# A hybrid decoder layer on one core: gate and up with another order of the seven products, longer lead of the adding transfers and one weight sum on VectorE

## Chip, cores and metric

One core of a Trainium2 chip. The metric is the device time of one execution of the whole kernel, in microseconds (us).

## The reference

One decoder layer over 512 tokens of width 2048, in float32. RMSNorm, an input projection, four token mixers side by side (two kinds of attention, a gated unit, RWKV-7), an output projection and a residual; then the part that the change is about, RMSNorm and a SwiGLU feed-forward of width 5632, and a final RMSNorm:

```python
def swiglu(h, w_gate, w_up, w_down):
    return (jax.nn.silu(h @ w_gate) * (h @ w_up)) @ w_down
...
        x = x + ycat.reshape(B, S, D_MIX) @ w_out[l]
        h = rmsnorm(x, norm_ffn_g[l])
        x = x + swiglu(h, w_gate[l], w_up[l], w_down[l])
    return rmsnorm(x, norm_final_g)
```

## The kernel before

Every product of float32 matrices is made of three matmuls on float32r parts: high times high, high times low, low times high. The high part is a rounded copy that ScalarE writes, the low part is what VectorE gets when it subtracts the high part from the value. `split2` (L1047, L1048) does both.

**Gate and up** are one product of 2 x 2 blocks in Strassen's manner (Winograd's form): the two halves of the tokens by the two halves of the model width, times the two halves of the width by gate and up. Seven products P1 to P7 stand for eight. Their activation operands (`cmb`) are sums of the four blocks of the normalised residual, made once while the output projection ends: `make_x2` adds the residual, `first_sums` and `last_sums` make sums and split them, `square_x2` and `add_squares` collect the squares for the norm, and what is not done by then comes from the generators `late_sums` and `ffn_norm`. The width of 5632 is worked in 11 groups (`gi`) of 512 columns of gate and of up. A group has 28 steps: seven products in the order of `ORDER` by four pieces `jj` of the inner dimension. A step is 2 inner tiles by 2 token tiles by 3 matmuls.

The weights' side is made as the products go. The queue of SP loads 512 KB pieces into X[jj] (tile T, four buffers, `w_dma`) for P1 and 256 KB pieces (tile wq) for P3 and P2. The sums of weight blocks that P5, P6, P4 and P7 need are made by transfers that add (`accum_op`), issued on POOL's queue by `w_add`: into X[jj] for P5, P6 and P4, into the raw tiles of P3 for P7. Each can start when the product before it on that tile has been split. `w_split` cuts a step's weight into high and low, `w_next` issues transfers and a split in order, `w_ahead` keeps the splits two steps ahead of the matmuls and the loads some steps more.

Products gather in PSUM. P6, P7 and P4 add onto the bank of P1, P3 adds onto that of P5, P2 has its own (`strassen`, dictionary `bank`). After the last matmul of a product `got_product` copies or adds the bank into tiles c11, c12, c21, c22. When gate and up of a token half are there it hands them to `turn_h`, a generator that gates (Silu by ScalarE, a product by VectorE), turns the result by transposes on TensorE, forms the operands of the down projection and stores them to DRAM from ScalarE's queue (`put`). Generators in `side` go one step on at each half-step of the matmuls (`run`, `step_side`), so where a `yield` stands decides beside which matmuls a piece of gating is issued. All engines work through their instructions in the order of issue.

The order before is P1 P5 P6 P3 P7 P4 P2. **The down projection** follows; two of its products are issued ahead of what is left of the gating, and its tiles take over the memory of the stage before.

## Time and profile before

| | us |
|---|---|
| median of 3 runs | 2351.08 |
| lowest and highest run | 2344.31, 2355.11 |
| the profiled execution | 2343.19 |
| span of the profiled execution, first to last instruction | 2341.5 |
| mean granted clock of TensorE over the span | 0.987 |

The times of single instructions below come from the profiled execution. A matmul's duration overlaps with those of its neighbours; its pace is the distance from start to start. The time that an engine sat idle before an instruction, and what ended it, stand behind the instruction.

### The profile page before, as it was taken

What the parts mean: (1) busy time and instruction counts of PE and PEld (TensorE: products, weight loads), DVE (VectorE), ACT (ScalarE), POOL (GpSimd) and SP (SyncE); (2) the same over time, 40 slices, a digit from 0 to 9 for tenths busy, and PEclk for the clock granted to TensorE, in tenths of its full rate; (3) what the DMA queues carried; (4) which work ended last, traced back from release to release, by engine and by line L of the source; (5) the groups of instructions that cost most, each with busy time, mean ns of one, the idle gap of its engine ahead of it and who ended that gap; (6) DMA issues with size and microseconds to landing.
All of it is one profiled execution on the core that took longest, in us unless ns stands there. A gap on an engine that the chain in (4) does not pass through costs nothing.

```text
span 2341.5 us, 29080 instructions
## 1 busy us (share of the span) xinstructions
PE 2240.9 (96%) x11064; PEld 1788.6 (76%) x11064; DVE 1357.1 (58%) x1950; ACT 1010.6 (43%) x1508; POOL 194.3 (8%) x236
## 2 busy tenths in 40 slices
PE   8999999999999997999999999999999889999996
PEld 6788878877777775777777777777777668888884
DVE  6555456654444456755555455555555577777775
ACT  5522222244444444544454454444445344443333
POOL 0000000000000000212211221221221100000000
PEclk9999999999999999999999999999999989999998
DMA  5232323122233334877977987797797587547884
GB/s 185 83 98 73 102 68 100 61 91 84 69 106 106 95 113 140 183 189 181 259 196 177 235 209 185 200 246 185 188 257 195 137 304 239 173 124 259 286 308 153
DMA packets 164541, 388.92 MB, mean 166 GB/s; under 512 B 29296, under 2 KB 34928, under 8 KB 164400
## 3 DMA queue, kind: packets, MB, share of 16 engines
q1 hardware_dynamic: 103728, 245.15, 31.8%
q0 software_dynamic: 31680, 92.29, 21.2%
q10 hardware_dynamic: 28992, 49.61, 6.1%
q8 instruction: 87, 1.43, 0.2%
q14 instruction: 54, 0.44, 0.1%
HBM read 348.93 MB, written 38.05 MB: 165 GB/s over the span
## 4 chain that ended last, share of the span: by engine, by line
PE 56%; issue 17%; DMA 12%; DVE 7%; ACT 4%; POOL 3%; ACTq 0%; SPq 0%; POOLq 0%; DVEq 0%
DMA T<-in_wgu_dram 8%; PE acc L145 7%; PE acc L147 7%; PE acc L146 7%; PE bk L1379 5%; PE bk L1380 5%; PE bk L1378 5%; PE acc L166 3%; PE acc L168 2%; PE acc L167 2%; DMA wq<-in_wgu_dram 2%; POOL wq L1141 2%; PE prod L1294 2%; PE prod L1295 2%; PE prod L1296 2%
## 5 line engine op out<-in xcount | busy, mean ns | idle before, releaser
L1048 DVE TENSOR_TENSOR wl<-T,wh 128x1024 fp32r<-128x1024 f32 x176 | 214.8, 1224 | 267.8 <-ACT wh L1047 265.5
L1295 PE MATMUL prod<-wl,h 128*128 128x512 f32 x704 | 278.3, 395 | 15.2 <-DVE wl L1048 14.6
L1047 ACT ACTIVATE wh<-T 128x1024 fp32r<-128x1024 f32 x176 | 185.9, 1059 | 236.4 <-DMA T<-in_wgu_dram 117.9
L1294 PE MATMUL prod<-wh,h 128*128 128x512 f32 x704 | 276.0, 392 | 1.6 <-ACT wh L1047 1.6
L1296 PE MATMUL prod<-wh,l 128*128 128x512 f32 x704 | 274.7, 390 | 0.0
L1378 PE MATMUL bk<-dh,ah 128*128 128x512 f32 x608 | 239.4, 394 | 25.0 <-ACT dh L1047 25.0
L1048 DVE TENSOR_TENSOR wl<-wq,wh 128x512 fp32r<-128x512 f32 x264 | 173.1, 689 | 135.4 <-ACT wh L1047 134.5
L1379 PE MATMUL bk<-dl,ah 128*128 128x512 f32 x608 | 239.5, 394 | 3.3 <-DVE dl L1048 3.3
L107 DVE TENSOR_TENSOR wlo<-wraw,whi 128x1024 fp32r<-128x1024 f32 x127 | 155.3, 1222 | 148.2 <-ACT whi L106 147.9
L1380 PE MATMUL bk<-dh,al 128*128 128x512 f32 x608 | 238.2, 392 | 0.0
L106 ACT ACTIVATE whi<-wraw 128x1024 fp32r<-128x1024 f32 x127 | 133.9, 1054 | 196.5 <-PE acc L146 94.1
L145 PE MATMUL acc<-xhi,whi 128*128 128x512 f32 x512 | 209.6, 409 | 5.4 <-ACT whi L121 5.1
L1047 ACT ACTIVATE wh<-wq 128x512 fp32r<-128x512 f32 x264 | 155.2, 625 | 134.7 <-PE prod L1296 75.2
L1143 POOL DMA_DIRECT2D T<-in_wgu_dram x132 | 118.1, 917 | 1140.9 <-DVE x L1036 588.5
L147 PE MATMUL acc<-xhi,wlo 128*128 128x512 f32 x512 | 201.1, 393 | 1.2 <-DVE wlo L107 1.2
L146 PE MATMUL acc<-xlo,whi 128*128 128x512 f32 x512 | 200.8, 392 | 0.3 <-DVE xlo L239 0.3
L1295 PEld LDWEIGHTS prod<-wl,h 128*128 128x128 f32 x704 | 132.1, 188 | 55.7 <-DVE wl L1048 29.0
L1294 PE MATMUL prod<-wh,hb 128*128 128x512 f32 x352 | 142.1, 404 | 18.7 <-DVE c L1265 18.7
L1294 PEld LDWEIGHTS prod<-wh,h 128*128 128x128 f32 x704 | 132.2, 188 | 31.5 <-ACT wh L1047 4.1
L1378 PEld LDWEIGHTS bk<-dh,ah 128*128 128x128 f32 x608 | 115.3, 190 | 50.5 <-ACT dh L1047 26.7
L1296 PEld LDWEIGHTS prod<-wh,l 128*128 128x128 f32 x704 | 132.2, 188 | 26.6
L1047 ACT ACTIVATE dh<-T 128x1024 fp32r<-128x1024 f32 x66 | 70.0, 1060 | 172.5 <-DVE T L1457 56.3
(315 smaller groups left out, 4128.6 us busy)
## 6 DMA issues: line engine op xcount, KB each, us to landing
rw<-in_wdn_dram SPq DMA_DIRECT2D x134, 512.0 KB, 4.9
T<-in_wgu_dram POOLq DMA_DIRECT2D x132, 512.0 KB, 9.6
wq<-in_wgu_dram SPq DMA_DIRECT2D x176, 256.0 KB, 5.7
wraw<-in_wi_dram SPq DMA_DIRECT2D x63, 512.0 KB, 3.6
T<-in_wgu_dram SPq DMA_DIRECT2D x44, 512.0 KB, 5.1
wq<-in_wgu_dram POOLq DMA_DIRECT2D x88, 256.0 KB, 9.1
wraw<-in_wt_dram SPq DMA_DIRECT2D x32, 512.0 KB, 3.6
wraw<-in_wo_dram SPq DMA_DIRECT2D x32, 512.0 KB, 3.6
```

The lines of the kernel that those rows point to most:

```text
L107: dv.tensor_sub(lo, r, hi.bitcast(F32))
L145: pe.matmul(acc[b], wh, xh, start=(c == 0 and k == 0), stop=False)
L146: pe.matmul(acc[b], wh, xl, start=False, stop=False)
L147: pe.matmul(acc[b], wl, xh, start=False, stop=(c == nchunk - 1 and k == 3))
L1047: ac.activation(hi, src, AF.Copy)
L1048: dv.tensor_sub(lo, src, hi.bitcast(F32))
L1294: pe.matmul(acc[t], ah[:, tt], hi[:, u], start=first, stop=False, skip_group_check=more)
L1295: pe.matmul(acc[t], ah[:, tt], lo[:, u], start=False, stop=False, skip_group_check=more)
L1296: pe.matmul(acc[t], al[:, tt], hi[:, u], start=False, stop=(j == 7), skip_group_check=more)
L1378: pe.matmul(o, ah[:, a], hi[:, cc], start=fresh, stop=False, skip_group_check=True)
L1379: pe.matmul(o, ah[:, a], lo[:, cc], start=False, stop=False, skip_group_check=True)
L1380: pe.matmul(o, al[:, a], hi[:, cc], start=False, stop=last, skip_group_check=True)
```

## The change

The products of gate and up run in the order P1 P2 P5 P3 P6 P7 P4. P6's weight sum is no longer a transfer: after P3's split VectorE adds P3's raw tiles to X. The transfers that add are issued 8 steps ahead of the split instead of 4, the loads 7 steps ahead of the matmuls instead of 8. P2 and P5 have banks of the pool `px`, P1 one of `pm`. c11 is complete after P2, c12 after P6, c22 after P7, c21 with P4, so that the first token half is gated beside P7 and the second beside P1 and P2 of the next group; `turn_h` makes and stores the operands of the down projection in another order and keeps the first half's blocks until the second half is there. On the activations' side the sums are split in interleaved pieces (`first_high`, `a11_high` and so on), the lower blocks (`lower_half`) come before the `last_sums`, and `ffn_norm` begins ten half-steps later.

```diff
-    def split_a11(j):
-        a11 = t2("a11", dt=F32R)
-        split2(a11[:, lo_t], xg[j][:, lo_t], a11[:, hi_t])
+    def a11_high(j):
+        a11 = cmb["P1", j] = t2("a11", dt=F32R)
+        ac.activation(a11[:, lo_t], xg[j][:, lo_t], AF.Copy)
+
+    def a11_low(j):
+        a11 = cmb["P1", j]
+        dv.tensor_sub(a11[:, hi_t], xg[j][:, lo_t], a11[:, lo_t].bitcast(F32))
         cmb["P1", j] = a11[:, lo_t], a11[:, hi_t]
...
     def late_sums():
         first_sums(7)
-        yield
-        for j in range(5, 8):
-            last_sums(j)
+        first_high(7)
+        yield
+        first_low(7)
+        for j in range(LOWER, 8):
+            lower_half(j)
+            yield
+        for j in range(8):
+            last_sums(j)
             yield
             yield
...
     def ffn_norm():
+        for _ in range(10):
+            yield
...
-    ORDER = ("P1", "P5", "P6", "P3", "P7", "P4", "P2")
+    ORDER = ("P1", "P2", "P5", "P3", "P6", "P7", "P4")
     LOADS = dict(P1=(0, 0), P3=(1, 1), P2=(1, 0))
-    ADDS = dict(P5=(0, 1), P6=(1, 1), P4=(1, 0), P7=(0, 1))
+    ADDS = dict(P5=(0, 1), P4=(1, 0), P7=(0, 1))
...
                 split2(hi[:, u], raw["P3", j] if p == "P3" else raw.pop(("P3" if p == "P7" else p, j)), lo[:, u])
+            if p == "P3":
+                for u in range(2):
+                    dv.tensor_add(X[jj][:, u], X[jj][:, u], raw["P3", 2 * jj + u])
...
-        w_add(sw["split"] + 4)
+        w_add(sw["split"] + 8)
...
-        w_dma(k + 8)
+        w_dma(k + 7)
...
         p = turned(0)
+        yield
         a = t2("hT")
         ac.activation(a, p, AF.Copy)
...
+        yield
+        p = turned(1)
+        yield
+        if th == 0:
+            put("P1", a)
+            b = t2("hT")
+            ac.activation(b, p, AF.Copy)
+            yield
+            hi = high("P2", b)
+            held[gi] = a, b
+            yield
+            put("P2", low(b, hi).bitcast(F32), 1)
             return
...
+        a11, a12 = held.pop(gi)
+        hi = high("P4", p)
+        s1 = t2("hs")
+        dv.tensor_add(s1, p, a)
+        yield
+        put("P5", s1)
+        put("P4", low(p, hi).bitcast(F32), 1)
+        yield
+        s3 = t2("hs")
+        dv.tensor_sub(s3, a11, a)
         yield
         hi = high("P7", s3)
-        dv.tensor_sub(s2, held.pop("S1"), a)
-        yield
-        put("P6", s2)
...
+        s2_ = t2("hs")
+        dv.tensor_sub(s2_, s1, a11)
+        yield
+        put("P6", s2_)
+        put("P7", low(s3, hi).bitcast(F32), 1)
+        yield
+        dv.tensor_sub(a12, a12, s2_)
+        put("P3", a12)
...
         if p == "P1":
             keep("c11")
+        elif p == "P2":
+            add("c11")
         elif p == "P5":
             keep("c22")
+        elif p == "P3":
+            keep("c12")
         elif p == "P6":
-            keep("c12")
-        elif p == "P3":
-            dv.tensor_add(part["c12", t], acc, part["c12", t])
+            add("c12")
+            gated(0, "c11", "c12")
         elif p == "P7":
-            dv.tensor_add(part["c22", t], acc, part["c22", t])
+            add("c22")
...
-            bank[key] = [(px if p == "P5" else pm)("prod") for _ in range(2)]
+            bank[key] = [(pm if p == "P1" else px)("prod") for _ in range(2)]
...
             if b:
-                split_a11(g)
                 if g:
                     first_sums(g - 1)
+                a11_high(g)
+                if g:
+                    first_high(g - 1)
+                a11_low(g)
+                if g:
+                    first_low(g - 1)
+                    add_squares()
...
-                if g == 6:
-                    for j in range(3):
-                        last_sums(j)
+                if g in (5, 6):
+                    for j in range(2):
+                        lower_half(2 * (g - 5) + j)
             elif g == 7:
-                for j in range(3, 5):
-                    last_sums(j)
+                lower_half(4)
```

## Rows read from the trace of the kernel before

**Rows 1.** Stretches: us, busy us (instructions) PE, PEld, DVE, ACT, POOL; clock, DMA share, GB/s

```profile
856.30:925.00 68.70, 63.59 (x263) 49.84 (x263) 41.73 (x67) 32.86 (x52) 0.00 (x0) 0.98 0.44 138
925.00:932.50 7.50, 0.00 (x0) 0.00 (x0) 4.39 (x9) 3.90 (x6) 0.00 (x0) 0.73 0.42 139
932.50:1022.30 89.80, 84.84 (x352) 67.15 (x353) 58.14 (x83) 47.33 (x70) 18.53 (x21) 0.95 0.74 161
...
1022.30:1860.50 838.20, 802.65 (x3522) 645.38 (x3520) 454.30 (x571) 394.93 (x551) 173.48 (x199) 0.99 0.84 206
1860.50:1881.70 21.20, 7.06 (x32) 5.18 (x32) 11.16 (x15) 5.65 (x8) 0.00 (x0) 0.82 0.67 234
```

**Rows 2.** Timeline, TensorE: start us, duration us, engine, line, operation, [idle before <-releaser]

```profile
1309.96 0.39 PE L1294 MATMUL prod<-wh,h 128*128 128x512 f32 x1
...
1326.96 0.39 PE L1294 MATMUL prod<-wh,h 128*128 128x512 f32 x1
```

**Rows 3.** Timeline: one set of transposes and the matmul behind it

```profile
1181.72 0.60 PE L1194 MATMUL ph<-cm,c 128*128 128x128 f32 x4
1182.08 0.48 PE L1294 MATMUL prod<-wh,hb 128*128 128x512 f32 x1
```

**Rows 4.** Waits of TensorE, 1022 to 1858 us: total us, times, longest us

```profile
PE prod L1294 <- DVE c L1265: 18.4, 10, 3.0
PE prod L1295 <- DVE wl L1048: 13.8, 29, 0.8
```

**Rows 5.** Waits of ScalarE, same stretch

```profile
ACT wh L1047 <- DMA T<-in_wgu_dram: 115.4, 58, 4.1
```

**Rows 6.** Transfer issues, 1000 to 1850 us: KB each, median us to landing

```profile
T<-in_wgu_dram POOLq DMA_DIRECT2D x120, 512.0 KB, 9.7
...
T<-in_wgu_dram SPq DMA_DIRECT2D x38, 512.0 KB, 5.1
```

**Rows 7.** Instructions by form, 1022.3 to 1860 us: busy us, mean ns | idle before

```profile
L1048 DVE TENSOR_TENSOR wl<-T,wh 128x1024 fp32r<-128x1024 f32 x159 | 194.2, 1224 | 255.9 <-ACT wh L1047 253.8
L1047 ACT ACTIVATE wh<-T 128x1024 fp32r<-128x1024 f32 x158 | 167.0, 1059 | 222.9 <-DMA T<-in_wgu_dram 115.4 <-PE prod L1296 47.9 <-DVE hs L1243 20.9
L1048 DVE TENSOR_TENSOR wl<-wq,wh 128x512 fp32r<-128x512 f32 x240 | 157.6, 689 | 124.7 <-ACT wh L1047 123.9
...
L1254 ACT ACTIVATE c<-prod 128x512 f32<-128x512 f32 x60 | 33.3, 589 | 14.9 <-PE prod L1296 13.8 <-issue 0.2
...
L1265 DVE TENSOR_TENSOR c<-prod,c 128x512 f32<-128x512 f32 x20 | 12.8, 682 | 0.0
```

**Rows 8.** Timeline: P7's last matmul and P4's first, first group

```profile
998.39 0.39 PE L1296 MATMUL prod<-wh,l 128*128 128x512 f32 x1
...
999.17 0.47 PE L1294 MATMUL prod<-wh,hb 128*128 128x512 f32 x1 [0.39 <-DVE c L1265]
```

**Rows 9.** Timeline: the same place in the fourth group

```profile
1249.38 1.28 DVE L1265 TENSOR_TENSOR c<-prod,c 128x512 f32<-128x512 f32 x2
...
1250.21 0.47 PE L1294 MATMUL prod<-wh,hb 128*128 128x512 f32 x1 [2.40 <-DVE c L1265]
```

**Rows 10.** Timeline: two low parts on VectorE and an issue on POOL

```profile
1544.16 2.41 DVE L1048 TENSOR_TENSOR wl<-T,wh 128x1024 fp32r<-128x1024 f32 x2 [0.96 <-ACT wh L1047]
...
1545.68 0.86 POOL L1143 DMA_DIRECT2D T<-in_wgu_dram  x1 [2.52 <-DVE wl L1048]
```

**Rows 11.** Waits of VectorE, 856 to 925 us

```profile
DVE a L1048 <- ACT a L1047: 7.7, 7, 1.1
DVE l L1048 <- ACT h L1047: 4.9, 7, 0.7
```

**Rows 12.** Timeline: the first last_sums' high part, the first matmul of gate and up

```profile
923.11 0.63 ACT L1047 ACTIVATE h<-s 128x512 fp32r<-128x512 f32 x1 [1.11 <-DVE s L1074]
...
932.50 0.80 PE L1294 MATMUL prod<-wh,a 128*128 128x512 f32 x1 [7.51 <-ACT wh L1047]
```

**Rows 13.** Timeline: TensorE goes on in the down projection

```profile
1881.74 0.80 PE L1378 MATMUL bk<-dh,ah 128*128 128x512 f32 x1 [12.50 <-ACT dh L1047]
```

More of the change, by code (lines that the diff above doesn't have):

```diff
@@ L1062, in first_sums, with first_high, first_low, lower_half @@
         dv.scalar_tensor_tensor(s12[:, hi_t], s12[:, lo_t], -1.0, a[:, lo_t], op0=OP.mult, op1=OP.subtract)
-        h12, l12 = t2("h12", dt=F32R), t2("l12", dt=F32R)
-        split2(h12, s12, l12)
-        cmb["P5", j] = h12[:, lo_t], l12[:, lo_t]
-        cmb["P6", j] = h12[:, hi_t], l12[:, hi_t]
-        dv.scalar_tensor_tensor(s12[:, lo_t], s12[:, hi_t], -1.0, b[:, lo_t], op0=OP.mult, op1=OP.subtract)
+    def first_high(j):
+        h12[j] = t2("h12", dt=F32R)
+        ac.activation(h12[j], s2[j], AF.Copy)
+    def first_low(j):
+        h, s12 = h12.pop(j), s2[j]
+        l12 = t2("l12", dt=F32R)
+        dv.tensor_sub(l12, s12, h.bitcast(F32))
+        cmb["P5", j] = h[:, lo_t], l12[:, lo_t]
+        cmb["P6", j] = h[:, hi_t], l12[:, hi_t]
+        dv.scalar_tensor_tensor(s12[:, lo_t], s12[:, hi_t], -1.0, xg[j + 8][:, lo_t], op0=OP.mult, op1=OP.subtract)
+    def lower_half(j):
+        hb, lb = t2("hb", dt=F32R), t2("lb", dt=F32R)
+        split2(hb, xg.pop(j + 8), lb)
+        cmb["P2", j] = hb[:, lo_t], lb[:, lo_t]
+        cmb["P4", j] = hb[:, hi_t], lb[:, hi_t]
     def last_sums(j):
@@ L1085, in late_sums, with ffn_norm @@
             yield
-        for j in range(8):
-            hb, lb = t2("hb", dt=F32R), t2("lb", dt=F32R)
-            split2(hb, xg.pop(j + 8), lb)
-            cmb["P2", j] = hb[:, lo_t], lb[:, lo_t]
-            cmb["P4", j] = hb[:, hi_t], lb[:, hi_t]
+    def ffn_norm():
+        for _ in range(10):
             yield
-            yield
-    def ffn_norm():
         while len(sqs) > 1:
@@ L1196, in turned @@
             return p
-        rn = [norm2.r[:, 2 * th + t:2 * th + t + 1] for t in range(2)]
+        rn, neg = ([x[:, 2 * th + t:2 * th + t + 1] for t in range(2)] for x in (norm2.r, norm2.neg))
         if th == 0:
@@ L1254, in keep, with add, gated @@
             ac.activation(part[name, t], acc, AF.Copy)
+        def add(name):
+            dv.tensor_add(part[name, t], acc, part[name, t])
+        def gated(th, g, u):
+            if t:
+                side.append(turn_h(gi, th, *([part.pop((n, t)) for t in range(2)] for n in (g, u))))
         if p == "P1":
             keep("c11")
+        elif p == "P2":
+            add("c11")
         elif p == "P5":
             keep("c22")
+        elif p == "P3":
+            keep("c12")
         elif p == "P6":
-            keep("c12")
-        elif p == "P3":
-            dv.tensor_add(part["c12", t], acc, part["c12", t])
+            add("c12")
+            gated(0, "c11", "c12")
         elif p == "P7":
-            dv.tensor_add(part["c22", t], acc, part["c22", t])
-        elif p == "P4":
+            add("c22")
+        else:
             part["c21", t] = t2("c21")
             ac.activation(part["c21", t], acc, AF.Silu, scale=norm2.r[:, 2 + t:3 + t])
-            if t:
-                side.append(turn_h(gi, 1, *([part.pop((n, u)) for u in range(2)] for n in ("c21", "c22"))))
-        else:
-            dv.tensor_add(part["c11", t], acc, part["c11", t])
-            if t:
-                side.append(turn_h(gi, 0, *([part.pop((n, u)) for u in range(2)] for n in ("c11", "c12"))))
+            gated(1, "c21", "c22")
     bank = {}
@@ L1304, in strassen @@
             del bank[key]
+    LOWER = 5
     for g in range(8):
```

37 lines of the change are left out of this document (4 added, 33 removed).

## The prediction

> **What bounds the kernel now.** I read the busy time and the granted clock by stretch first [rows 1]. The change touches four stretches: the end of the output projection, where the operands of gate and up are made (856.3 to 925.0 us), a stretch of 7.5 us in which TensorE runs nothing, the first group of gate and up (932.5 to 1022.3) and its ten other groups (1022.3 to 1860.5). Behind them the start of the down projection (1860.5 to 1881.7) depends on the gating that the change reorders. TensorE is the bound in all of them, so a gain can only come from time that it does not spend on matmuls.
>
> How long the matmuls take by themselves: in a stretch without waits 75 of them start between 1309.96 and 1326.96 us, 0.2267 us each [rows 2]. A group of gate and up has 28 steps of 12, 336 matmuls, 76.2 us, so a step is 2.72 us. Ten groups are 761.7 us. A group also turns its gated block with four sets of four transposes, and a set pushes the next matmul back by 0.45 us (due at 1181.72, came at 1182.08, and the one behind it 0.08 late) [rows 3], 18 us in ten groups. The stretch has 838.2 us [rows 1]. So 838.2 - 761.7 - 18 = 58.5 us are lost, **5.8 us a group**.
>
> Where they are lost, by the waits of TensorE [rows 4]: 18.4 us in ten waits for the c22 addition (L1265), which must have read its PSUM bank before P4 accumulates into the same bank; 13.8 us in 29 waits for the low part of a weight (L1048); the rest is the same two on the weight loads and the slower matmuls behind a stall. Most of this goes back to the accumulating transfers: ScalarE waited 115.4 us, 58 times, for them to land in T [rows 5]. Such a transfer takes 9.7 us from issue to landing, a plain one 5.1 [rows 6]. Today P5 and P6 follow four steps (10.9 us) behind the last reader of the sum. Of these the split takes 1.06 us (ScalarE) and 1.22 us (VectorE) [rows 7], which leaves 8.6 us for a transfer of 9.7. P4's sum is issued only four steps ahead and queues behind eight sums of P7 on POOL.
>
> One bank change shows both cases. In the first group, with VectorE free, the last matmul of P7 starts at 998.39, the next is due at 998.62 and comes at 999.17 [rows 8]: about 0.6 us lost with the slower one behind it. At 1250 us, in the fourth group, the splits had waited for their transfers, c22 came behind a late low part on VectorE, and TensorE idled 2.40 us [rows 9].
>
> **The change, part by part.** *Lead of the sums.* In the new order P5 stands 8 steps behind P1, P7 8 behind P3, P4 8 behind P6, and the adds are issued 8 steps ahead, so each has 21.8 us less 2.3 for the split and about 1 for the issue: 18 us against 9.7. The T waits of P5 and P4 should go. P6's 44 transfers leave POOL altogether, a quarter of its bytes in this stage. What is late next: the loads of P1's T, which need the buffer that P4 gives up only four steps earlier. They have 10.9 - 2.3 = 8.6 us on SP's queue against 5.1 [rows 6], and two steps of split-ahead behind that; P2's loads queue behind them on SP and still have about 5 us to spare. I take zero.
>
> The Trainium skill, "DMA: Bandwidth & Descriptors", section "Anatomy of one DMA", gives 2.0 us plus the bytes over 436 GB/s for a transfer issued by GpSimd; 512 KB would then be an estimated 3.2 us, four steps would be ample already, and a longer lead would be worth nothing. The trace disagrees, with 9.7 us [rows 6].
>
> *P6's sum on VectorE.* 88 additions of 128x512; the nearest row, the low part of a 128x512 weight, is 0.689 us [rows 7], so 5.5 us a group. They fall into the four steps that split P3, where VectorE then has 4 x 0.69 = 2.76 us of work against 2.72: full, but the split runs two steps ahead, and the backlog of some 1 us is worked off in P6, where a step costs 1.22. Cost taken 0; if the cover were gone, 0.7 us a step, 2.8 a group.
>
> The Trainium skill, "SBUF — State Buffer", warns that GpSimd cannot write the descriptors of its transfers while a VectorE instruction holds the port pair that they share. If instructions with two SBUF inputs, such as these additions, held it too, P7's sums would be issued up to four steps later and their slack would almost vanish; the chance of the second rival below would go from 0.12 to about a quarter. The trace speaks against it: a POOL issue of 0.86 us lies wholly inside such a VectorE pair [rows 10].
>
> *Order and banks.* P3 adds onto P5's bank and P6, P7, P4 onto P1's. Before, only P7 to P4 follow each other on one bank. After, P5 to P3, P6 to P7 and P7 to P4 do: three turnarounds in place of one. The one row with a free reader says 0.6 us [rows 8]. P6 to P7 and P7 to P4 have VectorE reading (0.682 us), P5 to P3 has ScalarE (0.589) [rows 7], so I take 0.6 + 0.6 + 0.5 = 1.7 us a group. Bounds for each: 0.3 (ScalarE answers at once) and 1.8, the mean of today's ten waits [rows 4]. I take the low row, since what made VectorE late there was the transfer.
>
> *Gating.* The second token half (th 1) now makes its sums in one run beside P1 and P2 of the next group. Its first transposes stand four half-steps behind P4's end, and the two Silu, a split of a full T and two multiplications must go before: about 0.65 us late by the durations. Its stores are issued from ScalarE right behind the VectorE subtraction they store, so ScalarE waits three or four times with the next split queued behind it. Adding the durations up, P5's first weight arrives just in time; I take 0.5 us a group, 0 to 2. Together: 1.7 + 0.65 + 0.5 = **2.9 us a group instead of 5.8, 29 us in ten groups** (bounds: 43 gained with 1.5 a group, 5 lost with 6.3).
>
> *End of the output projection.* VectorE waited 7.7 and 4.9 us there for the high parts from ScalarE [rows 11], 1.8 us a block. The new order puts the next block's sums into that time and saves about 1.2 us a block. Four blocks with one weight chunk are bound by this chain. The stretch has 68.7 us for 264 matmuls (59.8), 8.9 lost; I take 4 back, 0 to 8.
>
> *The empty 7.5 us.* VectorE makes three last_sums and then two more (the first high part at 923.11) before the first weight can be split, and TensorE starts at 932.50 [rows 12]. The new code has two pieces of lower_half in each of two blocks that have slack, and one at the end, 0.63 us of ScalarE [rows 12] and 0.69 of VectorE [rows 7], with no subtraction ahead of them. 6.5 of 7.5 us go, 0 to 7.5.
>
> *First group.* 89.8 us [rows 1] against 76.2 and two sets of transposes, 12.7 lost, mostly while VectorE makes the remaining operands. The work stays, the squares' additions move ten half-steps back onto P2 and P5, P2's operands now come first: 4 us back, 0 to 8.
>
> *Start of the down projection.* TensorE idles 12.50 us there [rows 13], because the tiles of the next pool wait for the stores of the last gating. That chain is now th 1's instead of th 0's, its Silu runs straight from PSUM, and it ends about 2 us sooner. I take 2; which buffers a store frees can shift it, so -5 to +6.
>
> **Sum.** 29 + 4 + 6.5 + 4 + 2 = 45.5 us. The profiled execution took 2343.2 us (span 2341.5 and 1.7 around it) and would take 2297.7. It lies 7.9 us under the median of the runs, 2351.1, so that the median becomes 2351.1 - 45.5, about **2305 us**.
>
> **Rivals.** *1, slower: the turnarounds meet a busy engine.* If each of the three costs as much as the longest wait for c22 today, 3.0 us [rows 4], because VectorE is behind with its additions or ScalarE stands at a store, a group loses 9 + 1.15 = 10.2 instead of 5.8: 44 us more, less 16.5 elsewhere: 2378. It decides from 2.0 us for each turnaround on (3 x 2.0 + 1.15 - 5.8, ten times, is about 14). For it: today's mean is 1.8. Against: that mean goes with late transfers. Chance 0.08. *2, no change: the transfers stay late*, because the DMA share of 0.84 [rows 1] and not the lead sets their 9.7 us, or since P1's loads take their place. Then 5.8 stays and two turnarounds come on top, 11 us lost against 16.5 gained: 2346. Chance 0.12. *3, more:* turnarounds of 0.3 and no stall from the stores, 43 us, and the other stretches near their bounds, 25: 2283. Chance 0.13. *4, it does nothing:* the lead of 8 alone could not help P5 today, since its sum is issued the moment P1 is split; with the new order it can, so this has no more than what rival 2 has.
>
> **How the numbers follow.** The forecast has 0.67, from 2295 to 2330. The range runs from 2277, a little under rival 3, to 2338, where a part of rival 2, transfers late by half, still lies. Faster by over 0.5% (about what a measurement here can tell from no change), under 2339: 0.67 + 0.13 + 0.03 of rival 2 = 0.83. Within 0.5%: the other 0.09. Slower: rival 1, 0.08.
>
> **What would show it.** Right: a group of about 80 us instead of 83.8; ScalarE's waits for T nearly gone; waits of TensorE for c22, for the c12 addition and for ScalarE's copy of P5, some 0.3 to 0.6 us each, eleven times each; the first matmul of P1 some 10 us earlier against the last of the output projection's start; POOL with 88 T issues. Wrong: waits of over 1.5 us at the turnarounds, low parts late in P3 or P5, ScalarE waiting for P1's T, or the granted clock falling behind a longer idle.

## The result, and the profile after

| us | before | after |
|---|---|---|
| median of the runs made side by side | 2347.74 (2344.31 to 2355.11) | 2289.79 (2289.41 to 2290.22) |
| the profiled execution | 2343.19 | 2289.41 |
| its span | 2341.5 | 2287.7 |
| mean granted clock of TensorE | 0.987 | 0.992 |

The ratio of the times is 0.9749, 95% interval 0.9722 to 0.9776: the changed kernel is faster by 2.5%. The forecast was 2305 us, its range 2277 to 2338. The saving was forecast at 45.5 us; the spans differ by 53.8. The windows of the kernel after cut it by the same stretches as [rows 1] (us; then busy us and instructions of PE, PEld, DVE, ACT and POOL; granted clock, DMA share, GB/s):

```profile
856.30:919.20 62.90, 60.86 (x263) 48.82 (x263) 43.87 (x70) 35.22 (x57) 0.00 (x0) 1.00 0.53 170
919.20:919.70 0.50, 0.21 (x2) 0.02 (x1) 0.24 (x2) 0.43 (x1) 0.00 (x0) 1.00 0.71 258
919.70:1012.00 92.30, 82.55 (x353) 65.26 (x354) 67.69 (x99) 48.05 (x72) 14.95 (x17) 0.98 0.63 145
1012.00:1809.40 797.40, 792.17 (x3522) 643.01 (x3521) 506.15 (x651) 397.25 (x562) 138.32 (x159) 1.00 0.78 190
1809.40:1828.30 18.90, 6.33 (x33) 5.11 (x32) 7.08 (x11) 4.13 (x7) 0.00 (x0) 0.79 0.58 194
```

With the exact first and last matmul of each part, the spans are accounted for like this:

| stretch | before | after | difference | forecast |
|---|---|---|---|---|
| end of the output projection | 69.9 | 64.4 | -5.6 | -4 |
| from its last matmul to the first of gate and up | 7.9 | 0.7 | -7.2 | -6.5 |
| first group | 89.8 | 92.3 | **+2.5** | **-4** |
| ten groups | 838.2 | 797.4 | **-40.8** | **-29** |
| start of the down projection | 21.2 | 18.9 | -2.3 | -2 |
| everything else | 1314.5 | 1314.0 | -0.4 | 0 |
| sum | | | -53.8 | -45.5 |

So two terms need an explanation: the ten groups gave 12 us more than forecast, and the first group lost time where a gain was forecast. The waits of TensorE and of its weight loads in the ten groups after (total us, times, longest us; the first row answers [rows 4]):

```profile
PE prod L1317 <- DVE c L1275: 3.9, 20, 0.2
...
PEld prod L1317 <- issue: 11.8, 20, 0.6
PEld prod L1317 <- ACT c L1272: 4.9, 14, 0.4
PEld ph L1216 <- DVE c L1226: 4.8, 10, 0.5
```

No low part of a weight is late any more, and the waits for additions are 20, all at a change of bank and none over 0.2 us. The waits of ScalarE there:

```profile
ACT wh L1047 <- PE prod L1319: 278.3, 193, 2.3
ACT c L1272 <- PE prod L1319: 36.8, 30, 1.8
ACT wh L1047 <- DMA wq<-in_wgu_dram: 19.6, 10, 2.0
ACT wh L1047 <- DVE hT L1265: 18.8, 10, 1.9
```

The 115.4 us for T of [rows 5] are gone. What ScalarE waits for now is TensorE, that is, a free buffer: it is ahead. Every group takes 79.7 us, where those before took 82 to 86.

The loss of a step is the time from the last matmul of the step before to its own last matmul, less the 2.72 us of the forecast, read from the timeline of TensorE; a change of bank so counts to the product behind it. The sums of each product's four steps, as means over the ten groups (us in a group, the four sets of transposes included):

| | P1 | P5 | P6 | P3 | P7 | P4 | P2 | sum |
|---|---|---|---|---|---|---|---|---|
| before | 0.83 | 1.75 | 1.50 | 0.00 | 0.00 | 2.57 | 0.97 | 7.62 |
| after | 1.31 | 0.00 | 0.00 | 0.31 | 1.47 | 0.48 | 0.00 | 3.56 |

### The profile page after: what moved, and what is told of

Read it like the earlier page. It is cut to its first block, busy times and chain, and to the rows that moved or that the text cites. A ratio compares the mean times of both kernels' runs of the same rounds, so it can differ in the third digit from the quotient of the medians.

```text
span 2287.7 us, 29132 instructions
## 1 busy us (share of the span) xinstructions
PE 2225.0 (97%) x11064; PEld 1783.3 (78%) x11064; DVE 1412.5 (62%) x2038; ACT 1011.3 (44%) x1519; POOL 155.6 (7%) x192
## 4 chain that ended last, share of the span: by engine, by line
PE 87%; DVE 6%; ACT 3%; issue 2%; DMA 1%; ACTq 0%; SPq 0%; DVEq 0%
PE prod L1317 11%; PE prod L1319 11%; PE prod L1318 11%; PE acc L145 8%; PE acc L147 7%; PE acc L146 7%; PE bk L1406 5%; PE bk L1407 5%; PE bk L1405 5%; PE acc L166 3%; PE acc L168 3%; PE acc L167 3%; ACT dh L1047 1%; DVE dl L1048 1%; PE ph L1216 1%
## 5 line engine op out<-in xcount | busy, mean ns | idle before, releaser
L1162 POOL DMA_DIRECT2D T<-in_wgu_dram x88 | 76.1, 865 | 964.1 <-DVE x L1036 575.6
```

## Experiments

The steps that the forecast rests on are tried first one part at a time, then the two terms that missed. All times are medians. Those of the kernel before spread over some 18 us, those of the changed kernel and its kin over 2 or 3; kernels of that kin with nothing to tell them apart (the first two below, *order_alone* and the kernel after) lie within 0.9 us of each other, so differences of 2 us and more between such kernels are read as differences, though they were not all run side by side.

### Is it the lead, the sum on VectorE, or the order?

**lead4** takes back the longer lead of the sums.

```diff
-        w_add(sw["split"] + 8)
+        w_add(sw["split"] + 4)
```

> The changed kernel with the adding transfers issued 4 steps ahead of their split instead of 8; order, banks, gating and P6's sum on VectorE stay. Theory A (the order of the products took the transfers off the path, and 8 steps are more than they need): 4 steps are 10.9 us, less about 1 us for the issue on POOL, against 8.4 us for a 512 KB sum and 5.8 us for a 256 KB one in the changed kernel; so the ten later groups stay at 79.7 us or lose under 1 us each, 2290 to 2298 us in all. Theory B (the lead of 8 is what matters, as the prediction put it together with the order): the waits of ScalarE for T come back, most of the 4.1 us a group that the ten groups gained goes, 2320 to 2335 us.

Measured: 2289.20 us (ratio to before 0.9727, 0.9704 to 0.975), 0.6 us under the kernel after, and groups of 79.7 us. The lead gives nothing.

**p6_transfer** takes back P6's sum on VectorE: it is a transfer again.

```diff
-    ADDS = dict(P5=(0, 1), P4=(1, 0), P7=(0, 1))
+    ADDS = dict(P5=(0, 1), P6=(1, 1), P4=(1, 0), P7=(0, 1))
...
-            if p == "P3":
-                for u in range(2):
-                    dv.tensor_add(X[jj][:, u], X[jj][:, u], raw["P3", 2 * jj + u])
```

> The changed kernel with P6's weight sum made by a transfer again (P5, P3, P6: 8 steps behind P5) and without VectorE's 88 additions. Theory A (the sum on VectorE was not what gained; both ways are hidden): the ten groups stay at 79.7 us each, the first group gains 1 to 3 us because VectorE is full there, 2286 to 2292 us. Theory B (fewer bytes by the adding queue shortened the landings from 9.7 to 8.4 us, and that cured the waits): the landings rise to 9.7 us again and the groups lose 1 to 4 us each, 2300 to 2330 us. Theory C (the additions cost time where P3 is split): a gain of up to 0.7 us a step, 2.8 a group, 2260 us.

Measured: 2290.08 us (0.973, 0.9709 to 0.975), groups of 79.7 us, and a first group that loses as much as after; the gain there that one theory expected did not come. The transfers of the two kernels over 800 us (KB each, median us from issue to landing), first after, then p6_transfer:

```profile
T<-in_wgu_dram POOLq DMA_DIRECT2D x80, 512.0 KB, 8.4
wq<-in_wgu_dram POOLq DMA_DIRECT2D x80, 256.0 KB, 5.8
```

```profile
T<-in_wgu_dram POOLq DMA_DIRECT2D x120, 512.0 KB, 8.4
...
wq<-in_wgu_dram POOLq DMA_DIRECT2D x80, 256.0 KB, 8.6
```

The 40 transfers more make P7's sums land 2.8 us later, and nobody waits for it: in this order both forms are covered.

**order_alone** takes back both, so that of the weights' side little but the order is left, with the banks and the gating that go with it (both edits above).

> The changed kernel with both of its other edits to the weights' side undone at once: the adding transfers are issued 4 steps ahead of their split and P6's sum is a transfer again. What is left is the order of the products, the banks and the gating that follow from it. Theory A (the order alone, by which each sum stands 8 steps behind the last reader of its tile, made the gain of the ten groups): 79.7 us a group, 2288 to 2292 us. Theory B (either edit would do without the other, since each alone made no difference): with 132 transfers of 512 KB on POOL and the short lead they crowd again as in the kernel before, ScalarE waits for T or wq, 1 to 4 us a group, 2300 to 2330 us.

Measured: 2289.89 us (0.9737, 0.971 to 0.9764), groups of 79.7 us. The whole gain of the ten groups comes from the order with its banks and gating. (The loads' lead of 7 steps, 8 before, also stays in every kernel of this kin; no run tried it alone.) A kernel with the new order and the old gating was not built, since the gating follows from which tile is complete when.

### Where the old order lost it

**p5_near** keeps the lead of 4 and puts P5 four steps behind P1 again, as before, with its sum's transfer; only P6's part is still done on VectorE.

```diff
-    ORDER = ("P1", "P2", "P5", "P3", "P6", "P7", "P4")
+    ORDER = ("P1", "P5", "P2", "P3", "P6", "P7", "P4")
```

> The changed kernel in the order P1 P5 P2 P3 P6 P7 P4 and with a lead of 4 (a longer one cannot be given to P5 here; the lead alone made no difference in lead4): P5's transfer stands 4 steps behind P1's split, the other sums 8 steps behind theirs, and P5 to P3 is no longer a change on one bank. Theory A (the distance is what counts): 10.9 us less 2.3 for the split and 1 for the issue against 8.4 of landing, so ScalarE waits for T at P5 and TensorE loses 0.5 to 1.5 us a group there, as at P5 of the kernel before, and gains 0.31 at P3: 2292 to 2303 us. Theory B (with the other transfers out of the way a sum lands soon enough at any distance): only the gain at P3 stays, 2285 to 2288 us.

Measured: 2287.14 us (0.9723, 0.9692 to 0.9753), groups of 79.4 us, the last 80.4. P5 loses nothing at a distance of four steps but for one step of the last group (1.03 us); its sums land within 8.5 us (median). The 0.31 us of the bank change from P5 to P3 are gone too, since P2 now stands between the two. So distance alone did not make P5 late before.

Read again with that in mind, the waits of ScalarE in the kernel before hold more rows than the prediction looked at (1022 to 1860 us; they stand below the one for T [rows 5]):

```profile
ACT wh L1047 <- PE prod L1296: 111.9, 81, 4.2
ACT wh L1047 <- DMA wq<-in_wgu_dram: 49.8, 56, 2.4
...
ACT wh L1047 <- DVE hs L1243: 20.9, 9, 2.3
ACT wh L1047 <- DVE hs L1219: 20.9, 9, 2.3
```

Put down product by product, the 115.4 us for T split into 69.3 at P6 and 46.1 at P4, and none at P5; the 49.8 us for wq are P7's sums. The time from issue to landing was 7.6 us in the median of all eleven groups for P5's sums, 9.5 for P6's, 9.1 for P7's and 13.4 (10.7 to 16.1) for P4's. Set against the start of the step that needs them (us, medians of 40 steps in the ten groups, from the issues and the timeline of TensorE; for P7 the second of a step's two sums):

| sum issued / landed ahead of its step | P5 | P6 | P7 | P4 |
|---|---|---|---|---|
| before | 13.8 / 5.7 | 12.2 / 2.7 | 13.4 / 3.5 | 19.9 / 6.0 |
| order_alone | 25.4 / 15.3 | 23.9 / 15.6 | 25.4 / 16.9 | 26.2 / 18.7 |
| p5_near | 14.5 / 6.1 | none | 23.6 / 17.6 | 26.3 / 18.1 |

A weight needs 2.3 us of splitting ahead of its step, and the split stands in a queue. Before, P6's sums landed 2.7 us ahead (1.2 at the least); in the new order nothing lands under 13 us ahead but P5 in p5_near, which has as little time as before and loses next to nothing.

P4's 6.0 us are no cover, since the start of P4 is itself late. The second group shows how (1080 to 1084 us):

```profile
1080.86 1.06 ACT L1047 ACTIVATE wh<-T 128x1024 fp32r<-128x1024 f32 x1 [1.40 <-DMA T<-in_wgu_dram]
1081.95 1.23 DVE L1048 TENSOR_TENSOR wl<-T,wh 128x1024 fp32r<-128x1024 f32 x1 [1.23 <-ACT wh L1047]
1083.09 1.28 DVE L1265 TENSOR_TENSOR c<-prod,c 128x512 f32<-128x512 f32 x2
...
1083.92 0.47 PE L1294 MATMUL prod<-wh,hb 128*128 128x512 f32 x1 [2.96 <-DVE c L1265]
```

The sum for P4's second step lands, ScalarE splits it, VectorE makes the low part and only then reads P7's bank for c22. In each of the ten groups that sum lands 0.10 to 0.11 us before the split begins, and c22 stands directly behind the low part. So the late sum sets the wait that TensorE has for c22, as the prediction had read it from the fourth group.

Ahead of splits for P1 and P5 ScalarE stood instead at two stores of the gating: `put` is issued behind the VectorE product that it stores, and the next split is queued behind it.

**before_late_stores** takes the kernel before and issues these two stores a half-step or more later.

```diff
-            put("P5", s1)
             lo = low(p, hi)
             yield
+            put("P5", s1)
+            yield
             put("P4", lo.bitcast(F32), 1)
...
-        put("P3", s4)
         lo = low(p, hi)
         yield
+        put("P3", s4)
+        yield
         put("P2", lo.bitcast(F32), 1)
```

> The kernel before, with the gating stores of P5 and P3 issued half a step or more later on ScalarE, so that ScalarE no longer reaches them ahead of VectorE's products. Theory A: in the kernel before ScalarE stood about 2.3 us at each of two stores a group (20.9 and 20.9 us in nine groups each), and this is what delays P5's split and then P6's sum and split; those waits go, with them P5's loss (0.48 + 0.66 us a group) and part of P6's 1.2 us, and 10 to 20 us are gained: 2331 to 2341 us. Theory B: the four sums of P5, P6, P7 and P4 crowd the adding queue, and the stores only fill time in which ScalarE would wait for a sum anyway: at most 4 us gained, 2344 to 2351 us, with ScalarE's waits for T longer by what its waits for the stores lose.

Measured: 2346.15 us against 2352.53 of the kernel before (0.9973, 0.9954 to 0.9993): 6 us gained, between the two theories and nearer B. The waits of ScalarE:

```profile
ACT wh L1047 <- PE prod L1298: 155.2, 110, 5.0
ACT wh L1047 <- DMA T<-in_wgu_dram: 117.7, 57, 3.8
...
ACT wh L1047 <- DVE sl L1187: 4.7, 2, 2.4
```

The 41.8 us at the stores are gone; 43 us more of waiting for a free buffer have come (155.2 against 111.9), and T costs what it did. P5 loses 1.09 us a group instead of 1.75. That is 0.66 of the 1.14 us that were expected. Of the 1.09 left, 0.49 is a set of transposes and 0.6 stays at P5's third step; ScalarE waits near there for another product of the gating (12.6 us in ten waits before, for `sl`), which no run changed. P6 loses 2.49 instead of 1.50 and P4 3.2 instead of 2.57 in the profiled execution, which is one of the slower of this kernel (2350.64 us) where that of before is one of the faster (2343.19), so these two are not compared closely. So the stores delayed P5's last step; P6 and P4 wait for transfers, and they do so without these stores.

**before_p4_early** takes the kernel before and issues P4's sum ahead of P7's, right behind the split of P6 that frees the tile, to see whether the bank change to P4 is cheap when its weight is there.

```diff
-            if p in ADDS:
+            if p in ADDS and p != "P4":
...
+        gi, p, jj = steps[sw["split"]]
+        if p == "P6":
+            kh, f = ADDS["P4"]
+            gp.dma_start(X[jj].rearrange("p u n -> p (u n)"), wgu[gi, kh, f, jj], accum_op=OP.add)
```

> The kernel before with one edit: the transfer that adds P4's block to X is issued right behind P6's split, ahead of P7's eight, instead of 4 steps ahead of P4's split and behind them. Order and banks stay. Theory A (the wait for c22 between P7 and P4 was long because the low part ahead of c22 on VectorE came late, and that because the transfer for P4 landed late): the wait falls from 1.7 us idle in the mean to the 0.4 of the first group, a group from 83.8 to 82 us, eleven groups give 17 to 20 us: span 2321 to 2325 us. Theory B (a turnaround costs that much on VectorE in any case, and the new order was cheap for another reason): no change, span 2341 us.

Measured: 2398.21 us (1.0207, 1.0188 to 1.0226), slower, and P4 still loses 2.6 us a group (about 2.15 at the change of bank in seven of the ten), though its own sums now land some 30 us ahead. With P7 late as well, it tells nothing of the bank change. It tells what P4's sum stood behind. The transfers of that kernel and ScalarE's waits there:

```profile
T<-in_wgu_dram POOLq DMA_DIRECT2D x116, 512.0 KB, 9.4
wq<-in_wgu_dram SPq DMA_DIRECT2D x147, 256.0 KB, 13.5
...
wq<-in_wgu_dram POOLq DMA_DIRECT2D x72, 256.0 KB, 15.2
...
ACT wh L1047 <- DMA wq<-in_wgu_dram: 143.5, 92, 3.5
...
ACT wh L1047 <- DMA T<-in_wgu_dram: 65.5, 30, 4.3
```

P7's sums, now behind P4's, land after 15.2 us instead of 9.1, the second of a step 1.2 us after the step's first matmul instead of 3.5 us ahead of it, and P7 loses about 5 us a group that it did not lose before. In the old order there is no room on this queue: what is moved ahead makes late what then stands behind.

### Can the three changes of bank be had for nothing?

**spread_banks** keeps the products that share a bank apart: P1 P2 P5 P6 P3 P7 P4. P3's raw tiles are loaded with P5 and added to X one step ahead of P6's split, and the adding transfers are issued right behind the split that frees their tile.

```diff
-    ORDER = ("P1", "P2", "P5", "P3", "P6", "P7", "P4")
+    ORDER = ("P1", "P2", "P5", "P6", "P3", "P7", "P4")
...
+        m = 0 if (q, jj) == ("P5", 3) else jj + 1 if q == "P6" and jj < 3 else None
+        if m is not None:
+            for u in range(2):
+                dv.tensor_add(X[m][:, u], X[m][:, u], raw["P3", 2 * m + u])
```

> The changed kernel in the order P1 P2 P5 P6 P3 P7 P4: P6 between P5 and P3, P3 between P6 and P7, so that of the three places where a product adds onto the bank of the one before it only P7 to P4 is left. P3's loads come with P5, VectorE adds them to X beside P6, each transfer that adds is issued right behind the split that it waits for, so P7's has 4 steps and P4's 12. Theory A (each turnaround costs what the trace of the changed kernel shows, 0.31 us behind P5 and 0.48 behind P6): the ten groups take 78.9 us instead of 79.7, all eleven gain 8 to 9 us, 2280 to 2283 us. Theory B (P7's 256 KB sums land too late with 4 steps, 10.9 us less the split against 5.8 us of landing): ScalarE waits for wq and the groups lose 1 to 2 us each, 2295 to 2305 us.

Measured: 2317.02 us (0.9845, 0.9823 to 0.9866), 27 us slower than the kernel after; groups of 81.3 to 82.5 us. Both theories missed. The two changes of bank at P3 and P7 did fall to 0.00 us, but P2, P5 and P6 lost 1.26, 1.27 and 0.69 us a group that they do not lose after. ScalarE's waits show why for P6 and P2:

```profile
ACT wh L1047 <- DVE T L1167: 93.1, 40, 2.6
ACT wh L1047 <- DMA wq<-in_wgu_dram: 31.6, 9, 5.1
```

P6's split waits for the addition just ahead of it on VectorE, and P2's loads come late because P3's tiles are held longer and SP's queue stands at full buffers (172.5 us of waiting there for tiles wq, 90.8 after). What holds P5 up was not looked into. A change of bank of 0.3 to 0.5 us is cheaper than any of the three.

### The stretch ahead of the groups

**old_sum_order** takes the kernel after and puts the sums back one behind the other in `on_last`, uninterleaved.

```diff
-                if g:
-                    first_sums(g - 1)
                 a11_high(g)
-                if g:
-                    first_high(g - 1)
                 a11_low(g)
                 if g:
+                    first_sums(g - 1)
+                    first_high(g - 1)
                     first_low(g - 1)
-                    add_squares()
                 square_x2(g)
                 square_x2(g + 8)
+                if g:
+                    add_squares()
```

> The changed kernel with the calls in the output projection's blocks in the old order: split of a11, then the sums of the block before with their split, the squares, the addition of squares. Theory A (the interleaved order gave the 5.6 us by which that stretch became shorter): the stretch goes back from 62.9 to between 67 and 69 us, and the start of gate and up gets 0 to 1 us later still; 2294 to 2297 us in all. Theory B (it came from elsewhere, such as the squares' place): 2290 us.

Measured: 2298.61 us (0.9785, 0.9766 to 0.9805), 8.8 us more than after. The stretch takes 70.5 us instead of 64.4, the gap behind it is 2.8 us instead of 0.7, the first group 93.7 instead of 92.3. Taking the interleaving back costs 6.1 us there, all of the 5.6 that the stretch had gained. Two things go with it: the run also puts the addition of squares behind the squares again, so the two are not told apart, and the granted clock of the stretch is 0.95 here, 1.00 after and 0.98 before [rows 1], so that part of the time is slower matmuls behind a stall.

**before_late_sums** takes the kernel before and moves its five early `last_sums` behind the start of gate and up, out of the empty 7.5 us.

```diff
-        for j in range(5, 8):
+        for j in range(8):
             last_sums(j)
...
-                if g == 6:
-                    for j in range(3):
-                        last_sums(j)
-            elif g == 7:
-                for j in range(3, 5):
-                    last_sums(j)
```

> The kernel before with one edit: the five last_sums that stood ahead of gate and up come with the other three behind its start. Theory A (they alone kept the first weight's split back, and what they cost later is hidden or nearly): the empty 7.5 us fall to about 1.5, the first group grows by 0 to 2 us, 4 to 6 us gained, span 2335 to 2337. Theory B (VectorE has the same work before P3 either way and the first group is full): the first group grows by as much as the gap shrinks, span 2340 to 2342.

Measured: 2353.33 us, no change (1.0012, 0.9996 to 1.0028). The gap closes from 7.9 to 0.4 us, and the first group grows from 89.8 to 95.7:

```profile
925.30:1021.00 95.70, 85.66 (x352) 67.27 (x353) 63.31 (x93) 50.11 (x75) 18.50 (x21) 0.95 0.71 157
```

So 5.9 of the 7.5 us come back in the first group, but not all beside the moved work. P5 and P6 lose 3.6 us more there and P1 1.6 less, while 3.8 us more are lost at P4, where c22 now waits as in the other groups; in the kernel before this wait was 0.4 us in the first group:

```profile
PE prod L1294 <- DVE c L1265: 2.6, 1, 2.6
```

P4's sum was late there too: its first split waited 3.2 us for T. The ten groups took 12.6 us longer as well, P4's late sums above all; executions of this kernel differ by that much. What the moved `last_sums` cost by themselves is thus nearer 2 us than 5.9 in this execution, but the medians show no gain at all.

**late_squares** takes the kernel after and has the additions of squares start 22 half-steps later, two per half-step, with the norm right behind them.

```diff
     def ffn_norm():
-        for _ in range(10):
+        for _ in range(32):
             yield
         while len(sqs) > 1:
             add_squares()
-            yield
-        for _ in range(8):
+            add_squares()
             yield
```

> The changed kernel with the additions of the squares issued two at each half-step of the first group's P6 instead of one at each half-step from P2's second step on; the waiting half-steps behind them are left out. Theory A (in the first group VectorE has 1.22 us of split, 1.1 of last_sums and 1.4 of squares in a step of 2.72 us during P5, and that is why the first group became longer): the losses of P5 and P3 in the first group, 6.9 and 2.0 us, go, the first group takes 84 to 86 us instead of 92.3, 2281 to 2284 us in all. Theory B (the first group waits for last_sums' turn between VectorE and ScalarE or for P2's loads): 2288 to 2291 us.

Measured: 2289.82 us (0.9729, 0.9709 to 0.975), nothing gained. P5 and P3 lose 4.5 us instead of 8.9 in the first group, but P6 loses 5.6 instead of nothing: TensorE, which sums the squares over the partitions for the norm, reached them before VectorE did (start us, us, engine, line, instruction, idle before it).

```profile
983.92 1.05 PE L215 MATMUL pacc<-ones,sq 128*128 128x1 f32 x8 [2.79 <-DVE sq L1031]
984.84 0.49 PE L1316 MATMUL prod<-wh,h 128*128 128x512 f32 x1
```

**late_squares2** leaves three half-steps between the additions and the norm.

```diff
-        for _ in range(10):
+        for _ in range(31):
             yield
         while len(sqs) > 1:
             add_squares()
+            add_squares()
             yield
-        for _ in range(8):
+        for _ in range(3):
             yield
```

> The changed kernel with the additions of the squares two at a half-step at the end of P3 and the beginning of P6 of the first group, and three half-steps between them and the norm's matmuls; in late_squares TensorE stood 2.8 us before those matmuls because nothing lay between. Theory A (VectorE's load in P5 costs the first group its gain): P5 and P3 of the first group lose 4.5 us instead of 8.9 as in late_squares, and the 5.6 us that P6 lost there go; first group 87 to 89 us, span 2282.5 to 2285. Theory B (whatever is put off comes back in full): span 2287.7.

Measured: 2284.85 us (2284.35 to 2285.75; 0.9726, 0.9707 to 0.9745), 4.9 us under the kernel after. The first group is 88.2 us instead of 92.3. The instructions of VectorE beside four steps of P5, first after (945 to 961 us), then late_squares2 (944 to 960; busy us, mean ns, idle before and its releaser):

```profile
L1031 DVE TENSOR_TENSOR sq<-sq 128x512 f32<-128x512 f32 x8 | 5.5, 687 | 0.1
L1048 DVE TENSOR_TENSOR wl<-T,wh 128x1024 fp32r<-128x1024 f32 x4 | 4.9, 1218 | 0.0
L1048 DVE TENSOR_TENSOR l<-s,h 128x512 fp32r<-128x512 f32 x4 | 2.8, 692 | 2.8 <-ACT h L1047 2.8
```

```profile
L1048 DVE TENSOR_TENSOR wl<-T,wh 128x1024 fp32r<-128x1024 f32 x4 | 4.9, 1222 | 0.8 <-ACT wh L1047 0.8
L1048 DVE TENSOR_TENSOR l<-s,h 128x512 fp32r<-128x512 f32 x5 | 3.5, 692 | 3.5 <-ACT h L1047 3.5
```

Eight additions of squares, 5.5 us, stood among four weights that P5 needs one per 2.72 us.

### Both together

**best** is the kernel after with p5_near's order and lead and late_squares2's squares.

> The changed kernel with the order P1 P5 P2 P3 P6 P7 P4, transfers four steps ahead, and the norm's squares added two per half-step. Theory A: the two gains lie in different stretches (0.31 us of turnaround in each group; 4.9 us of the first group) and add: 2289.8 - 2.7 - 4.9 = about 2282 us. Theory B: P5 now follows P1 in the first group, so that its steps meet the squares that were moved away from the later products, and the first group gives back 3 to 5 us: 2285 to 2288 us.

Measured: 2282.23 us (2280.36 to 2283.38; 0.9703, 0.9679 to 0.9726), 7.6 us under the kernel after, which is 4.9 and 2.7 added up. Its windows, the first group and the ten others:

```profile
922.40:1009.60 87.20, 82.11 (x352) 63.98 (x353) 67.57 (x99) 48.01 (x72) 14.98 (x17) 1.00 0.72 164
1009.60:1803.30 793.70, 788.62 (x3520) 643.90 (x3519) 504.96 (x651) 394.61 (x562) 138.60 (x159) 1.00 0.79 191
```

## Why the prediction was right, and where it was not

**The total** was right within its range and 15 us high against the median measured, 2289.8 (15.8 by the unrounded sum, 2305.6). Of these, 3.4 are the reference: the saving was set against a median of 2351.1, while the kernel before ran at 2347.7 beside the changed one. 8.3 are the saving itself, 53.8 us of span instead of 45.5: the ten groups gave 11.8 more, the first group 6.5 less, the rest together 3.0 more. The last 4 come from the profiled execution of before, which lies 4.6 us under the median of those runs, while that of after lies within 0.4 us of its own. That the two misses have opposite signs and cancel in part is luck.

**The ten groups: right in kind, mis-sized in three terms.** The prediction put 2.9 us a group on the new order without transposes; it is 79.74 - 76.17 - 1.8 = 1.8.

- *Changes of bank*, taken as 0.6 + 0.6 + 0.5 = 1.7 from the one row with a free reader [rows 8], measured 0.48 (P6 to P7) + 0.48 (P7 to P4) + 0.31 (P5 to P3) = 1.27. The row of before held 0.39 us of idle time; after, the idle time is 0.20 at each change that VectorE reads:

```profile
1147.50 0.39 PE L1319 MATMUL prod<-wh,l 128*128 128x512 f32 x1
1148.09 0.47 PE L1317 MATMUL prod<-wh,h 128*128 128x512 f32 x1 [0.20 <-DVE c L1275]
...
1159.82 0.39 PE L1319 MATMUL prod<-wh,l 128*128 128x512 f32 x1
1160.40 0.47 PE L1317 MATMUL prod<-wh,hb 128*128 128x512 f32 x1 [0.20 <-DVE c L1275]
```

  From 1147.50 to 1148.09 are 0.59 us where a matmul's pace is 0.23: 0.36 at the start of the first, and 0.1 more because the matmuls behind it are slower. The bounds of 0.3 to 1.8 held, the low end was nearer. The row of before misled because its reader was not free. There c22's addition started right behind a low part, 0.62 us after the last matmul that it had to wait for (997.71); after, VectorE is idle and starts 0.43 us behind that matmul (1159.13). Before, then after:

```profile
997.19 1.23 DVE L1048 TENSOR_TENSOR wl<-T,wh 128x1024 fp32r<-128x1024 f32 x1 [1.49 <-ACT wh L1047]
998.34 1.28 DVE L1265 TENSOR_TENSOR c<-prod,c 128x512 f32<-128x512 f32 x2
```

```profile
1159.56 1.37 DVE L1275 TENSOR_TENSOR c<-prod,c 128x512 f32<-128x512 f32 x2 [0.20 <-PE prod L1319]
```

- *Late transposes of th 1*, taken as 0.65, cost 0.33.
- *Stores*, taken as 0.5 (0 to 2), cost nothing. (The 0.17 us that are left over: a set of transposes costs 0.49 rather than 0.45.) ScalarE still waits 18.8 us for hT (L1265), ten times, but its splits run ahead by then, as its 278 us of waiting for TensorE show.

Part of what the old order lost was the clock. Behind the wait for c22 the granted clock was 0.50, the lower level of 1.2 GHz, in three of the ten groups before, and 22 matmuls started 0.43 us apart instead of 0.23: 4.4 of the 40.8 us. After, no matmul of the ten groups ran at that level. The prediction had this in its 58.5 us as "the slower matmuls behind a stall", without a price. Two of the three places (columns as in [rows 1]):

```profile
1334.70:1338.00 3.30, 3.30 (x9) 2.62 (x8) 0.68 (x1) 0.00 (x0) 0.00 (x0) 0.50 0.88 312
...
1836.50:1839.80 3.30, 3.30 (x9) 2.60 (x8) 1.15 (x1) 0.00 (x0) 0.00 (x0) 0.50 0.83 310
```

**The transfers: right for P6, P7 and P4, wrong for P5.** The prediction gave each sum 18 us in the new order where P5 and P6 had 8.6 for a transfer of 9.7, and the "T waits of P5 and P4" were to go. That the new order gives more time is what the table above shows: P5's, P6's and P7's sums are issued 24 to 25 us ahead of their step instead of 12 to 14, P4's 26 instead of 20. But 9.7 is a median over products that land very differently. P5's sums came in time before, and ScalarE never waited for T there; P5 was late in its last step because of the stores (*before_late_stores*, 0.66 us a group; another 0.6 at its third step has no run), and a distance of four steps is enough for it (*p5_near*). The waits for T were P6's and P4's, those for wq P7's. Whether P6, P7 or P4 needs the longer distance most is open: no run changed one of these alone in the new order.

**The lead of eight** was credited with part of the slack and is worth nothing (*lead4*): P5's, P7's and P4's sums are issued 25.4, 24.0 and 26.2 us ahead of their step with a lead of four, and 25.4, 24.0 and 26.3 with eight, so something other than the lead sets their issue. POOL runs nothing but these sums in the ten groups (199 instructions [rows 1], 159 after), in the order of the steps whatever the lead, and what it waits for is mostly VectorE's low part, that is, the split that frees the tile (326.8 us, 68 times, for T after). The Trainium skill, "DMA: Bandwidth & Descriptors", section "Anatomy of one DMA", as the prediction had cited it, would also have made the lead worthless, by an estimated 3.2 us for 512 KB. That conclusion came true, but not for that reason: the same transfers take 8.4 us here in the median, and four steps were not ample in the old order.

**P6's sum on VectorE** was costed at nothing and cost nothing, nor did it bring anything (*p6_transfer*). The POOL issues in the new order, with these additions beside them (us busy, mean ns, idle before):

```profile
L1160 POOL DMA_DIRECT2D wq<-in_wgu_dram x80 | 70.2, 996 | 283.0 <-DVE T L1176 271.8 <-ACT c L1272 8.7 <-ACT wh L1047 2.5
L1162 POOL DMA_DIRECT2D T<-in_wgu_dram x80 | 69.0, 863 | 375.0 <-DVE wl L1048 352.3 <-DMA wq<-in_wgu_dram 18.6 <-DMA T<-in_wgu_dram 4.1
```

In *p6_transfer*, the same order without these additions, they took 979 and 863 ns by the same view, so the additions lengthened them by 17 ns and by nothing. The Trainium skill, "SBUF — State Buffer", section "SBUF: two separate sides", says that GpSimd cannot write descriptors while VectorE runs in a mode that uses the shared port pair. The prediction weighed whether instructions with two SBUF inputs do the same; these means show no sign of it.

**First group: the step that failed.** Forecast 4 us better, measured 2.5 worse. The prediction said that "the work stays, the squares' additions move ten half-steps back onto P2 and P5" and counted this as a gain, without adding up what VectorE has to do there. In P5 it is, per step, a weight's low part 1.22, a `last_sums` of 0.42 + 0.69 with 0.70 of waiting for ScalarE between them, and two additions of squares 1.37: 4.4 us against 2.72 (by the timeline, where they overlap a little, 4.19 from one low part of a weight to the next). P5 lost 1.41 + 1.47 + 2.53 + 1.49 us. Without the squares there the group takes 88.2 us instead of 92.3 (*late_squares2*): 4.1 of the 6.5 us that separate forecast and measurement. Of these 4.1, P2, P5, P3 and P6 together give 2.8. The other 1.3 lie in P1, ahead of the squares, where the granted clock was 0.50 after and 1.00 in *late_squares2*; what that owes to the edit is open. The same stretch in both (columns as in [rows 1]):

```profile
926.10:929.40 3.30, 3.03 (x7) 2.45 (x8) 2.51 (x5) 1.06 (x2) 1.73 (x2) 0.50 0.98 214
```

```profile
926.10:929.40 3.30, 2.55 (x11) 1.87 (x12) 2.92 (x4) 0.97 (x2) 1.48 (x2) 1.00 0.96 191
```

The remaining 2.4 us are not settled. The `last_sums`, all eight of which now lie in this group, are the nearest suspect: in *late_squares2* P5 and P3 still lose 4.5 us, and between two weights' low parts in P5, 3.21 us apart (946.83 and 950.04), VectorE has nothing but one `last_sums` with its wait of 0.70 us for ScalarE. The clock even hid some of the miss: the group's mean granted clock rose from 0.95 [rows 1] to 0.98, and some 16 matmuls at the lower level became 6, about 2 us at 0.2 us each.

**The other stretches** came as worked out: the end of the output projection gave 5.6 (forecast 4, 0 to 8) and the gap 7.2 (6.5). Whether closing the gap gains anything hangs on what the moved work meets: moving only the `last_sums` closed it by 7.5 us and left the median where it was (*before_late_sums*), a bound that the prediction should have had for gap and first group together. The start of the down projection gave 2.3 (2).

**Rivals.** Rival 1 (changes of bank at 2.0 us and more) did not occur, the longest wait for an addition being 0.2 us. Rival 2 (transfers stay late) did not: ScalarE does not wait for T. The result lies between the forecast and rival 3 (2283 us), nearer to rival 3, whose first condition, changes of bank near 0.3 us and stores at nothing, is about what happened.

## What to carry to other kernels

When several adding transfers on one queue serve several products, take the landing time for each product apart: a median over them hid that one was in time and another landed 6 us later, and gave the wrong reason to one of them. Where generators move work beside the matmuls, add up what the receiving engine must do in each step there against the step's length, the moved work included; the sum of 4.4 us against 2.72 could have been added up from rows of the kernel before. Before taking a price from "a row with a free reader", look at what the reader did just ahead of it. An engine's wait may stand in place of another (41.8 us at stores became 43 us for buffers): only what the next engine loses counts.

## What the hardware showed beyond that

A change of PSUM bank with its reader free cost TensorE 0.46 to 0.50 us with VectorE reading (20 of 20) and 0.31 to 0.35 with ScalarE (10 of 10), 0.1 us of the former in slower matmuls behind the idle 0.20. The same adding transfer of 256 KB took from 5.8 us (after) over 8.6 (*p6_transfer*) to 15.2 (*before_p4_early*) from issue to landing, and plain loads of 256 KB on SP's queue 5.8 in the kernel before and 13.5 in *before_p4_early*, which moves the same bytes with the sums in another order. Seventeen executions of the kernel before spread over 18 us (2342.8 to 2361.2), with mean granted clocks from 0.987 down to 0.981, the lowest in the slowest; four of the kernel after spread over 0.8 us at 0.991 and 0.992.
